# Sixteen experts: loads issued in rotation of twelve places, the tensor engine's groups in a fixed order, the branch behind them marked

## The chip, the cores and the metric

One core of one Trainium2 chip. The metric is the device time of one execution in microseconds (us); the kernel before took 1063.79 us, the median of three runs.

## The reference, cut to what matters

A first block (retention, a recurrent unit, a feed-forward part) and a second block (three attentions, a hierarchical mixture of experts) over 256 tokens of width 1024. The change lies in the last part of the second block, the experts. Each of 256 tokens goes to 2 of 16 experts; an expert has three weights, 1024x256 (gate), 1024x256 (up) and 256x1024 (down), all in float32:

```python
hid = silu(einsum('nd,edf->nef', hf, w_gate)) * einsum('nd,edf->nef', hf, w_up)
hid = hid * combine[..., None]
out = einsum('nef,efd->nd', hid, w_down)
```

`combine` holds the weights of the two chosen experts and zero elsewhere.

## The kernel before, in words

Everything up to the router is one long run of matmuls on TensorE; it ends at about 912 us. What follows is `experts`. Tokens are gathered into 64 places per expert (`SLOTS`), and experts are worked in eight pairs p = 0 to 7 (one expert on the left 64 columns of the array, the other on the right).

The work of TensorE falls into groups, each a small function: `gather(h)` (L1449; 32 matmuls that gather the tokens of eight experts, h = 0 or 1), `up(p)` (L1491; gate and up of a pair), `places` (L1472; once), `turn(p)` (L1505 and L1507; transposes), `down(p)` (L1520), `back(p)` (L1534 and L1535; eight matmuls that spread a pair's result over the tokens, each pair of them followed by an addition on VectorE into `y`, L1537). Between `up` and `turn` stands `act_up` (L1498 on ScalarE, L1499 on VectorE); behind `turn` a copy on ScalarE (L1509) that `down` reads; behind `down` the split of its result into two parts, a copy on ScalarE (L298) and a subtraction on VectorE (L299), which `back` reads. The tiles of that split have four buffers, as many as one pair needs. After the last `back` the four quarters of `y` are stored (L1539).

The program is written with a scheduler that lists each engine's instructions anew: what is traced first has priority, but an instruction that the scheduler believes ready earlier is put ahead. Nothing else orders the groups in the kernel before. Once listed, each engine runs its instructions strictly in that order, and so does the queue of SyncE (SP), which issues all loads: a load that waits for its place holds up all loads behind it.

The weights come in 48 loads of 1 MB, numbered here 0 to 47 in the order of use (the code's index less `FIRST`), each as two transfers of 512 KB into the two halves of a place. `up(0)` takes loads 0 to 3; from p = 1 on `up(p)` takes four and `down(p-1)` two: 4 to 7, 8 and 9, 10 to 13, 14 and 15, and so on; `down(7)` takes 46 and 47. Loads 0 to 4 are fetched long ahead into tiles of the pool `big`. The others take places in a rotation of thirteen written in `load` (L244): three in the pool `raw`, three in `hi`, three in `lo`, four in `big`. So loads 5 to 13 are fetched before the experts begin, 14 to 17 want a `big` tile, 18 to 20 `raw`, 21 to 23 `hi`. `get_raw` (L281) traces a load right where its matmuls are traced. The pool `big` has eleven tiles; when the experts begin, six others hold `pl`, `xt`, `xth`, `xtl` and the two halves of `xg[0]`; later `xg[1]` wants two and `y` one.

Ahead of the experts the router's arithmetic runs on VectorE. Meanwhile `busy` (L1330) lets TensorE repeat a matmul whose result nobody uses, `WAIT[0]` = 36 times and then `WAIT[1]` = 5 times. Behind the experts a count is read (L1412) and a branch (`tc.If`, L1413) steps over a fallback for experts with more than 64 tokens; the inputs here don't enter it.

Of the kernel before, what the change touches and what calls it, by code (L numbers as in the profile page):

```python
# [6 lines left out]
F32 = mybir.dt.float32  # L7
# [6 lines left out]
P = 128  # L14
D = 1024
KT = 8
SEQ = 256
# [9 lines left out]
HALF = 1024  # L27
RAW, SPL, BIG, AHEAD, RAWLI, WARM = 6, 6, 11, 2, 1, 10
PRE = (1, 1, 1, 1, 1, 0, 0, 0)
WAIT = (36, 5)  # L30
SLOTS = 64

OFF1 = dict(q=0, k=1024, v=2048, g=3072, li=4096, lg=5120, ga=6144, gb=7168)
# [91 lines left out]
PLAN = _plan()  # L125
FIRST = next(i for i, (key, _) in enumerate(PLAN) if key[0] == "eu")
# [71 lines left out]
class _Build:  # L198
    def __init__(self, nc, tc, ctx, a):
        self.nc, self.tc, self.a = nc, tc, a  # L200
        pool = lambda name, bufs, **kw: ctx.enter_context(tc.tile_pool(name=name, bufs=bufs, **kw))
        self.rawp, self.lop, self.hip = pool("raw", RAW), pool("wlo", SPL), pool("whi", SPL)
        self.cp, self.big, self.tmp = pool("cst", 1), pool("big", BIG), pool("tmp", 2)
        self.sml = pool("sml", 2)
        self.psum = pool("psum", 4, space=bass.MemoryType.PSUM)
        self.cur, self.emitted, self.split, self.raw, self.turn = 0, 0, {}, {}, 0
        self.ahead = AHEAD
        self.running = []
        self.n = 0
# [28 lines left out]
    def load(self, i, big=False):  # L238
        if i in self.raw:
            return  # L240
        pool = None
        if i >= FIRST and not big:

            pool = ("raw", "raw", "raw", "hi", "hi", "hi", "lo", "lo", "lo", "big", "big", "big", "big")[self.turn % 13]  # L244
            self.turn += 1
            big = pool == "big"
        both = self.bigt(shape=(P, 2, HALF)) if big else None
        self.raw[i] = []
        for h, (off, n) in enumerate(PARTS[i]):
            raw = both[:, h, :] if big else None  # L250
            if pool in ("hi", "lo"):
                raw = (self.hip if pool == "hi" else self.lop).tile([P, HALF], F32, name=self.name("exp"), tag=pool)
            self.raw[i].append(self.load_part(off, n, raw))
# [27 lines left out]
    def get_raw(self, *key):  # L281

        i = self.cur
        assert PLAN[i][0] == key and self.emitted == i
        self.cur = self.emitted = i + 1
        self.load(i)
        return self.raw.pop(i)

    def run_ahead(self, n):
# [1030 lines left out]
    def moe(self, xt, xs, logits, squares, keep):  # L1320
# [55 lines left out]
        def table():  # L1376
# [31 lines left out]
            v.tensor_copy(tab[:, :, 16:18], r3.unsqueeze(2).to_broadcast([P, 2, 2]))  # L1408
            self.split_act(tabs[:, :, 0, :], tabs[:, :, 1, :], tab)

        y = self.experts(xt, None, xs, tabs, place, table)
        n = nc.values_load(count[0:1, 0:1], min_val=0, max_val=SEQ)  # L1412
        with ExitStack() as deeper:  # L1413
            for i in range(1, SEQ // SLOTS):
                deeper.enter_context(self.tc.If(n > SLOTS * i))
                self.cur = self.emitted = FIRST
                xth, xtl = self.bigt(F32R, (P, 2, D)), self.bigt(F32R, (P, 2, D))
                for t in range(2):
                    self.split_act(xth[:, t, :], xtl[:, t, :], xt[:, t, :])
                rest = self.s(32, tag="rest")  # L1420
                v.tensor_scalar(rest, place, -float(SLOTS * i), None, op0=ALU.add)
                self.experts(y, y, (xth, xtl), tabs, rest)

    def experts(self, base, y, xs, tab, place, table=None):
# [2 lines left out]
        ident = self.c("ident")  # L1427
        NP, W = NEXP // 2, 8 * SLOTS
        pl = self.bigt(F32R, (P, 2, NEXP * SLOTS))

        def slots(h):
            for t in range(2):
# [7 lines left out]
        xg = {}  # L1440

        def gather(h):
            xg[h] = [self.bigt(shape=(P, 4, W)) for _ in range(2)]
            for k in range(KT):
                ps = self.mm()
                n = 0
                for t in range(2):
                    for x in xs:
                        te.matmul(ps, x[:, t, k * P:k * P + P], pl[:, t, h * W:h * W + W], start=n == 0, stop=n == 3)  # L1449
                        n += 1  # L1450
                dst = xg[h][k // 4][:, k % 4, :]
                if k % 2:
                    v.tensor_scalar(dst, ps, self.p("gffn", k), None, op0=ALU.mult)
                else:
                    act.mul(dst, ps, self.p("gffn", k))

        last = slots(0)
        gather(0)
        if table:
            with self.tc.issue_after(last.ins):  # L1460
                slots(1)
# [5 lines left out]
        def places():  # L1467

            pw = self.sp()
            for p in range(NP):  # L1470
                for t in range(2):
                    te.matmul(pw[:, 36 * p:36 * p + 36], pl[:, t, p * P:p * P + P], tab[:, t, :, :], start=t == 0, stop=t == 1)  # L1472
            pw4 = pw[:, 0:288].rearrange("p (a i e) -> p a i e", a=8, i=2)
            act.copy(cc[:, 0:144].rearrange("p (a e) -> p a e", a=8), pw4[:, :, 1, :])
            for j, half in enumerate((slice(0, SLOTS), slice(SLOTS, P))):
                v.tensor_tensor(cw[half, :], pw[half, 0:304].rearrange("p (a e) -> p a e", a=8)[:, :, j],
                                cc[half, :].rearrange("p (a e) -> p a e", a=8)[:, :, j], op=ALU.add)
            v.tensor_tensor(cr, pw4[:, :, 0, 16], cc[:, 0:144].rearrange("p (a e) -> p a e", a=8)[:, :, 16], op=ALU.add)
# [3 lines left out]
        def up(p):  # L1482

            ps = self.mm()
            h, o = p // 4, (p % 4) * P
            for i in range(4):
                ws = self.get_raw("eu", p, i)
                for kc in range(2):
                    k = 2 * i + kc
                    for j, w in enumerate(ws):  # L1490
                        te.matmul(ps[j * SLOTS:j * SLOTS + SLOTS, :],  # L1491
                                  xg[h][k // 4][:, k % 4, o + j * SLOTS:o + j * SLOTS + SLOTS],
                                  w[:, kc * 512:kc * 512 + 512], start=k == 0, stop=k == KT - 1)
            return ps

        def act_up(p, ps):
# [5 lines left out]
        def turn(p):  # L1502
            th, pt = hid.pop(p), self.sp()
            for b in range(2):
                te.transpose(pt[:, b * P:b * P + P], th[:, b * P:b * P + P], ident)  # L1505
            for t in range(2):
                te.transpose(pt[:, SEQ + t * P:SEQ + t * P + P], pl[:, t, p * P:p * P + P].bitcast(F32), ident)  # L1507
            hf, pb = self.t(SEQ), self.t(SEQ, F32R)
            act.copy(hf, pt[:, 0:SEQ])  # L1509
            v.tensor_copy(pb, pt[:, SEQ:512])  # L1510
            hid[p], back_[p] = hf, pb

        def down(p):
            hf = hid.pop(p)
            pd = [self.mm() for _ in range(2)]
            for k in range(2):
                ws = self.get_raw("ed", p, k)
                for b in range(2):
                    for j, w in enumerate(ws):
                        te.matmul(pd[b][j * SLOTS:j * SLOTS + SLOTS, :], hf[:, k * P + j * SLOTS:k * P + j * SLOTS + SLOTS],  # L1520
                                  w[:, b * 512:b * 512 + 512], start=k == 0, stop=k == 1)
            outs[p] = []
            for b in range(2):
                oh, ol = self.t(512, F32R), self.t(512, F32R)
                self.split_act(oh, ol, pd[b])
                outs[p].append((oh, ol))

        def back(p, y):

            pb = back_.pop(p)  # L1530
            for b, (oh, ol) in enumerate(outs.pop(p)):
                for t in range(2):
                    ps = self.sp()
                    te.matmul(ps, pb[:, t * P:t * P + P], oh, start=True, stop=False)  # L1534
                    te.matmul(ps, pb[:, t * P:t * P + P], ol, start=False, stop=True)  # L1535
                    c = slice(b * 512, b * 512 + 512)
                    v.tensor_tensor(y[:, t, c], ps, (base if p == 0 else y)[:, t, c], op=ALU.add)  # L1537
                    if p == NP - 1:
                        nc.sync.dma_start(self.a["out"][t * P:t * P + P, c], y[:, t, c])  # L1539

        for p in range(NP + 1):
            if p < NP:
                ps = up(p)
                if p == 0:
                    places()
                act_up(p, ps)
            if p == 1:
                gather(1)
            if p == 2 and y is None:
                y = self.bigt(shape=(P, 2, D))  # L1550
            if p:
                turn(p - 1)
            if 2 <= p < NP:
                back(p - 2, y)
            if p:
                down(p - 1)
        back(NP - 2, y)
        back(NP - 1, y)
        return y


# [76 lines left out]
```

## Time and profile before

| what | us |
|---|---|
| median of three runs (1061.39 to 1063.85) | 1063.79 |
| the profiled execution | 1061.6 |
| its span, first to last instruction | 1059.8 |
| TensorE busy | 1041.5 (98%) |
| experts, from the first matmul of `gather(0)` to the span's end | 913.4 to 1059.8 |

How to read it: instructions of one engine run one after another; an entry of the chain of waits is work or a wait that the end of the program hangs on. A matmul's end is modelled, so the start of the next is what tells, and TensorE's busy share is an upper bound. `L1491` is line 1491. PEld is the loading of a matmul's stationary operand, SPq, PEldq and so on are the sequencers of the engines.

### The profile page before, as it was taken

What the parts mean: (1) busy time and instruction counts of PE and PEld (TensorE: products, weight loads), DVE (VectorE), ACT (ScalarE), POOL (GpSimd) and SP (SyncE); (2) the same over time, 40 slices, a digit from 0 to 9 for tenths busy, and PEclk for the clock granted to TensorE, in tenths of its full rate; (3) what the DMA queues carried; (4) which work ended last, traced back from release to release, by engine and by line L of the source; (5) the groups of instructions that cost most, each with busy time, mean ns of one, the idle gap of its engine ahead of it and who ended that gap; (6) DMA issues with size and microseconds to landing.
All of it is one profiled execution on the core that took longest, in us unless ns stands there. A gap on an engine that the chain in (4) does not pass through costs nothing.

```text
span 1059.8 us, 19451 instructions
## 1 busy us (share of the span) xinstructions
PE 1041.5 (98%) x7806; PEld 938.2 (89%) x7806; DVE 688.8 (65%) x1271; ACT 521.9 (49%) x928; POOL 36.9 (3%) x58
## 2 busy tenths in 40 slices
PE   9999999999999999999999999999999999999995
PEld 8999998899999999999999899999989999753332
DVE  7798977576776666576697466787567675423333
ACT  6578454464455444455575556565456553221101
POOL 3200000000000000000101000000000000000000
PEclk9999999999999999999999999999999999999998
DMA  8644563356555555566427643545555476359981
GB/s 326 231 155 164 181 210 111 119 159 200 179 181 183 190 183 171 183 186 198 139 81 218 191 148 121 198 141 181 182 174 180 130 289 252 146 181 416 412 340 43
DMA packets 57474, 203.32 MB, mean 192 GB/s; under 512 B 6416, under 2 KB 7824, under 8 KB 57248
## 3 DMA queue, kind: packets, MB, share of 16 engines
q1 hardware_dynamic: 57232, 201.91, 55.8%
q8 instruction: 63, 1.03, 0.4%
q14 instruction: 35, 0.29, 0.1%
q10 hardware_dynamic: 144, 0.09, 0.0%
HBM read 200.92 MB, written 1.05 MB: 191 GB/s over the span
## 4 chain that ended last, share of the span: by engine, by line
PE 96%; DMA 1%; DVE 1%; ACT 1%; issue 0%; SPq 0%; POOL 0%; DVEq 0%; ACTq 0%; POOLq 0%
PE mm L342 23%; PE mm L341 23%; PE mm L343 23%; PE mm L1491 5%; PE mm L1520 3%; PE mm L380 2%; PE mm L382 2%; PE mm L381 2%; PE mm L1449 1%; PE sp L402 1%; DMA big<-w 1%; PE sp L1534 1%; PE sp L639 1%; PE sp L640 1%; PE sp L1535 1%; PE mm L523 1%
## 5 line engine op out<-in xcount | busy, mean ns | idle before, releaser
L341 PE MATMUL mm<-big,hi 128*128 128x256 f32 (+1 forms) x2024 | 576.0, 285 | 0.0
L342 PE MATMUL mm<-big,hi 128*128 128x256 f32 (+1 forms) x2024 | 571.9, 283 | 0.0
L343 PE MATMUL mm<-big,lo 128*128 128x256 f32 (+1 forms) x2024 | 570.4, 282 | 0.0
L268 ACT ACTIVATE hi<-raw 128x1024 fp32r<-128x1024 f32 (+1 forms) x279 | 292.6, 1052 | 293.3 <-PE mm L342 163.7
L269 DVE TENSOR_TENSOR lo<-raw,hi 128x1024 fp32r<-128x1024 f32 (+1 forms) x279 | 338.6, 1215 | 119.1 <-ACT hi L268 115.8
L341 PEld LDWEIGHTS mm<-big,hi 128*128 128x128 f32 x2024 | 381.8, 189 | 1.7 <-issue 1.0
L342 PEld LDWEIGHTS mm<-big,hi 128*128 128x128 f32 x2024 | 381.8, 189 | 0.7 <-DVE big L302 0.2
L343 PEld LDWEIGHTS mm<-big,lo 128*128 128x128 f32 x2024 | 382.2, 189 | 0.0
L396 POOL TENSOR_TENSOR sml<-sml,keep 128x2 f32<-128x2 f32 (+4 forms) x17 | 19.4, 1142 | 675.6 <-DVE sml L841 189.9
L1537 DVE TENSOR_TENSOR big<-sp,big 128x512 f32<-128x512 f32 x32 | 20.3, 684 | 19.9 <-PE sp L1535 19.9
L1498 ACT ACTIVATE tmp<-mm,sml 128x256 f32<-128x256 f32 x8 | 3.8, 473 | 56.1 <-PE mm L1491 56.1
L380 PE MATMUL mm<-hi,big 128*128 128x512 f32 (+1 forms) x80 | 29.9, 374 | 0.0
L382 PE MATMUL mm<-lo,big 128*128 128x512 f32 (+1 forms) x80 | 29.7, 372 | 0.0
L381 PE MATMUL mm<-hi,big 128*128 128x512 f32 (+1 forms) x80 | 29.6, 370 | 0.0
L1491 PE MATMUL mm<-big,big 128*64 128x512 f32 x112 | 27.7, 598 | 0.0
L298 ACT ACTIVATE tmp<-mm 128x512 fp32r<-128x512 f32 x16 | 9.2, 596 | 35.1 <-PE mm L1520 35.1
L299 DVE TENSOR_TENSOR tmp<-mm,tmp 128x512 fp32r<-128x512 f32 x16 | 10.8, 690 | 23.4 <-ACT tmp L298 23.2
L1491 PE MATMUL mm<-exp,big 128*64 128x512 f32 x96 | 23.7, 596 | 0.0
L1499 DVE SCALAR_TENSOR_TENSOR tmp<-mm,sml,tmp 128x256 f32<-128x256 f32 x8 | 3.9, 483 | 30.4 <-ACT tmp L1498 30.4
L298 ACT ACTIVATE big<-tmp 128x256 fp32r<-128x256 f32 x46 | 18.2, 407 | 5.8 <-DVE tmp L689 3.2
L1491 PEld LDWEIGHTS mm<-big,big 128*64 128x64 f32 x112 | 7.9, 136 | 14.9 <-issue 14.2
L1491 PEld LDWEIGHTS mm<-exp,big 128*64 128x64 f32 x96 | 7.1, 137 | 13.8 <-issue 13.2
(391 smaller groups left out, 1139.4 us busy)
## 6 DMA issues: line engine op xcount, KB each, us to landing
raw<-w SPq DMA_DIRECT2D x289, 512.0 KB, 3.6
exp<-w SPq DMA_DIRECT2D x38, 512.0 KB, 10.1
big<-w SPq DMA_DIRECT2D x34, 512.0 KB, 10.0
raw<-w SPq DMA_DIRECT2D x16, 448.0 KB, 3.2
big<-xT SPq DMA_DIRECT2D x4, 272.0 KB, 4.5
big<-xT SPq DMA_DIRECT2D x1, 1024.0 KB, 5.8
big<-memT SPq DMA_DIRECT2D x1, 1024.0 KB, 5.7
out<-big SPq DMA_DIRECT2D x4, 256.0 KB, 4.1
```

Source lines behind the costliest of these rows:

```text
L268: nc.scalar.activation(hi[:, :n], raw[:, :n], AF.Copy)
L269: nc.vector.tensor_tensor(lo[:, :n], raw[:, :n], hi[:, :n].bitcast(F32), op=ALU.subtract)
L298: nc.scalar.activation(hi, src, AF.Copy)
L341: nc.tensor.matmul(ps[:m, :n], wh, rh, start=k == 0, stop=False)
L342: nc.tensor.matmul(ps[:m, :n], wh, rl, start=False, stop=False)
L343: last = nc.tensor.matmul(ps[:m, :n], wl, rh, start=False, stop=k == nt - 1)
L380: nc.tensor.matmul(ps[:, :w], xh[:, k, c], wh, start=k == 0, stop=False)
L381: nc.tensor.matmul(ps[:, :w], xl[:, k, c], wh, start=False, stop=False)
L382: nc.tensor.matmul(ps[:, :w], xh[:, k, c], wl, start=False, stop=k == last)
L1491: te.matmul(ps[j * SLOTS:j * SLOTS + SLOTS, :], xg[h][k // 4][:, k % 4, o + j * SLOTS:o + j * SLOTS + SLOTS], w[:, kc * 512:kc * 512 + 512 ...
L1520: te.matmul(pd[b][j * SLOTS:j * SLOTS + SLOTS, :], hf[:, k * P + j * SLOTS:k * P + j * SLOTS + SLOTS], w[:, b * 512:b * 512 + 512], start= ...
L1537: v.tensor_tensor(y[:, t, c], ps, (base if p == 0 else y)[:, t, c], op=ALU.add)
```

## The change

Five things. Rotation: `load` uses twelve places in place of thirteen (three `big` in place of four), and `get_raw` traces not only its own load but all up to eleven ahead. Order: every group of TensorE's is traced inside `issue_after` of the group before it, which lets the scheduler put its matmuls nowhere but behind the last one of that group; it is an order of issue and adds no wait. The sequence itself is that of the loop before but for the end: `turn(7)` comes ahead of `down(6)`, and `down(7)` ahead of `back(6)`. `gather(0)` is traced after the table of weights in place of before it. Marking: `mark_branch_hint_location("done")` ahead of the experts and a label on the branch. Filling: `WAIT[0]` is 31 in place of 36. The line that sets `turn` and `ring` inside the branch belongs to the fallback and is not run.

```diff
-WAIT = (36, 5)
+WAIT = (31, 5)
...
-            pool = ("raw", "raw", "raw", "hi", "hi", "hi", "lo", "lo", "lo", "big", "big", "big", "big")[self.turn % 13]
+            pool = ("raw", "raw", "raw", "hi", "hi", "hi", "lo", "lo", "lo", "big", "big", "big")[self.turn % self.ring]
...
-        self.load(i)
+        for j in range(i, min(len(PLAN), i + self.ring) if i >= FIRST else i + 1):
+            self.load(j)
...
+        self.tc.mark_branch_hint_location("done")
         y = self.experts(xt, None, xs, tabs, place, table)
...
-                deeper.enter_context(self.tc.If(n > SLOTS * i))
+                deeper.enter_context(self.tc.If(n > SLOTS * i, label="done" if i == 1 else None))
                 self.cur = self.emitted = FIRST
+                self.turn, self.ring = 0, 9
...
         last = slots(0)
-        gather(0)
         if table:
...
-        for p in range(NP + 1):
-            if p < NP:
-                ps = up(p)
-                if p == 0:
-                    places()
-                act_up(p, ps)
+        def then(f, *args):
+            if not chain:
+                return f(*args)
+            with self.tc.issue_after(chain[-1].ins):
+                return f(*args)
+
+        then(gather, 0)
+        for p in range(NP):
+            ps = then(up, p)
+            if p == 0:
+                then(places)
+            act_up(p, ps)
             if p == 1:
-                gather(1)
+                then(gather, 1)
             if p == 2 and y is None:
                 y = self.bigt(shape=(P, 2, D))
             if p:
-                turn(p - 1)
-            if 2 <= p < NP:
-                back(p - 2, y)
+                then(turn, p - 1)
+            if p > 1:
+                then(back, p - 2, y)
+            if p == NP - 1:
+                then(turn, p)
             if p:
-                down(p - 1)
-        back(NP - 2, y)
-        back(NP - 1, y)
+                then(down, p - 1)
+        then(down, NP - 1)
+        then(back, NP - 2, y)
+        then(back, NP - 1, y)
```

Each group function now ends with `chain.append(mm)`, mm being its last matmul.

## Rows read from the trace of the kernel before

**Rows 1.** Busy time by stretch: start:end, length, engines, then clock, DMA share, GB/s.
```profile
921.00:928.00 7.00, 7.00 (x33) 2.21 (x32) 0.75 (x1) 0.00 (x0) 0.00 (x0) 1.00 0.00 0
...
980.80:993.70 12.90, 12.90 (x64) 5.17 (x60) 4.63 (x9) 2.04 (x4) 0.00 (x0) 1.00 1.03 413
```

**Rows 2.** Chain of waits, first groups: start us, us, engine and line.
```profile
913.38 7.70 PE mm L1449 x32
921.08 7.02 PE mm L1491 x32
928.10 1.89 PE sp L1472 x16
929.99 7.02 PE mm L1491 x32
937.00 7.65 PE mm L1449 x32
```

**Rows 3.** The same chain, a pair whose groups stand unbroken.
```profile
980.82 6.87 PE mm L1491 x32
987.69 0.37 PE sp L1505 x2
988.06 0.22 PE sp L1507 x2
988.28 0.23 PE sp L1534
...
990.13 3.58 PE mm L1520 x16
```

**Rows 4.** The same chain, where groups are broken up, and its last down.
```profile
1006.61 2.57 PE mm L1491 x10
...
1016.94 1.92 PE mm L1491 x8
...
1019.25 0.37 ACT tmp L1509
...
1045.67 1.96 PE mm L1520 x8
```

**Rows 5.** Waits of the load queue, 880 to 1062: total us, times, longest.
```profile
SPq L258 <- PE mm L1491: 20.3, 8, 16.4
```

**Rows 6.** Timeline of loads and of the matmuls that waited: start, us, engine.
```profile
933.60 4.24 SPq L258 DMA_DIRECT2D raw<-w  x6
...
951.91 6.88 SPq L258 DMA_DIRECT2D big<-w  x8
...
959.70 5.70 PE L1520 MATMUL mm<-big,tmp 128*64 128x512 f32 x16 [0.74 <-DMA big<-w]
```

**Rows 7.** The page: an issue's KB and its median us to landing.
```profile
raw<-w SPq DMA_DIRECT2D x289, 512.0 KB, 3.6
```

**Rows 8.** Timeline of the filling and of the selection that ends it.
```profile
909.02 3.12 PE L1330 MATMUL mm<-big 128*128 128x256 f32 x24
...
911.13 0.19 DVE L1361 TENSOR_TENSOR keep<-tmp 128x32 fp32r<-128x32 f32 x1
...
911.98 0.17 PE L1366 MATMUL sp<-keep,keep 128*128 128x16 f32 x1
```

**Rows 9.** Timeline of the end.
```profile
1048.24 1.29 DVE L299 TENSOR_TENSOR tmp<-mm,tmp 128x512 fp32r<-128x512 f32 x2 [0.96 <-ACT tmp L298]
...
1049.52 2.48 DVE L1537 TENSOR_TENSOR big<-sp,big 128x512 f32<-128x512 f32 x4
```

**Rows 10.** Lines 1539 and 1413: ns min/median/max, first and last start us.
```profile
L1539 SPq DMA_DIRECT2D out<-big x4: 338/868/1602, 1050.2 to 1052.9; - x4
...
L1413 SPq EVENT_SEMAPHORE  x8: 17/17/17, 1057.8 to 1058.4; - x8
...
L1413 PEldq COMPARE_BRANCH  x1: 3858/3858/3858, 1050.2 to 1050.2; - x1
...
L1413 DVEq EVENT_SEMAPHORE  x1: 21/21/21, 1055.8 to 1055.8; - x1
```

More of the change, by code (lines that the diff above doesn't have):

```diff
@@ L205, in __init__ @@
         self.psum = pool("psum", 4, space=bass.MemoryType.PSUM)
-        self.cur, self.emitted, self.split, self.raw, self.turn = 0, 0, {}, {}, 0
+        self.cur, self.emitted, self.split, self.raw, self.turn, self.ring = 0, 0, {}, {}, 0, 12
         self.ahead = AHEAD
@@ L1429, in experts @@
         pl = self.bigt(F32R, (P, 2, NEXP * SLOTS))
+        chain = []
         def slots(h):
@@ L1448, in gather @@
                     for x in xs:
-                        te.matmul(ps, x[:, t, k * P:k * P + P], pl[:, t, h * W:h * W + W], start=n == 0, stop=n == 3)
+                        mm = te.matmul(ps, x[:, t, k * P:k * P + P], pl[:, t, h * W:h * W + W], start=n == 0, stop=n == 3)
                         n += 1
@@ L1455, in gather @@
                     act.mul(dst, ps, self.p("gffn", k))
+            chain.append(mm)
         last = slots(0)
-        gather(0)
         if table:
@@ L1471, in places @@
                 for t in range(2):
-                    te.matmul(pw[:, 36 * p:36 * p + 36], pl[:, t, p * P:p * P + P], tab[:, t, :, :], start=t == 0, stop=t == 1)
+                    mm = te.matmul(pw[:, 36 * p:36 * p + 36], pl[:, t, p * P:p * P + P], tab[:, t, :, :], start=t == 0,
+                                   stop=t == 1)
+            chain.append(mm)
             pw4 = pw[:, 0:288].rearrange("p (a i e) -> p a i e", a=8, i=2)
@@ L1490, in up @@
                     for j, w in enumerate(ws):
-                        te.matmul(ps[j * SLOTS:j * SLOTS + SLOTS, :],
-                                  xg[h][k // 4][:, k % 4, o + j * SLOTS:o + j * SLOTS + SLOTS],
-                                  w[:, kc * 512:kc * 512 + 512], start=k == 0, stop=k == KT - 1)
+                        mm = te.matmul(ps[j * SLOTS:j * SLOTS + SLOTS, :],
+                                       xg[h][k // 4][:, k % 4, o + j * SLOTS:o + j * SLOTS + SLOTS],
+                                       w[:, kc * 512:kc * 512 + 512], start=k == 0, stop=k == KT - 1)
+            chain.append(mm)
             return ps
@@ L1506, in turn @@
             for t in range(2):
-                te.transpose(pt[:, SEQ + t * P:SEQ + t * P + P], pl[:, t, p * P:p * P + P].bitcast(F32), ident)
+                mm = te.transpose(pt[:, SEQ + t * P:SEQ + t * P + P], pl[:, t, p * P:p * P + P].bitcast(F32), ident)
+            chain.append(mm)
             hf, pb = self.t(SEQ), self.t(SEQ, F32R)
@@ L1519, in down @@
                     for j, w in enumerate(ws):
-                        te.matmul(pd[b][j * SLOTS:j * SLOTS + SLOTS, :], hf[:, k * P + j * SLOTS:k * P + j * SLOTS + SLOTS],
-                                  w[:, b * 512:b * 512 + 512], start=k == 0, stop=k == 1)
+                        mm = te.matmul(pd[b][j * SLOTS:j * SLOTS + SLOTS, :],
+                                       hf[:, k * P + j * SLOTS:k * P + j * SLOTS + SLOTS],
+                                       w[:, b * 512:b * 512 + 512], start=k == 0, stop=k == 1)
+            chain.append(mm)
             outs[p] = []
@@ L1534, in back @@
                     te.matmul(ps, pb[:, t * P:t * P + P], oh, start=True, stop=False)
-                    te.matmul(ps, pb[:, t * P:t * P + P], ol, start=False, stop=True)
+                    mm = te.matmul(ps, pb[:, t * P:t * P + P], ol, start=False, stop=True)
                     c = slice(b * 512, b * 512 + 512)
@@ L1539, in back @@
                         nc.sync.dma_start(self.a["out"][t * P:t * P + P, c], y[:, t, c])
-        for p in range(NP + 1):
-            if p < NP:
-                ps = up(p)
-                if p == 0:
-                    places()
-                act_up(p, ps)
+            chain.append(mm)
+        def then(f, *args):
[9 more added lines that the diff above has]
+            act_up(p, ps)
             if p == 1:
-                gather(1)
+                then(gather, 1)
             if p == 2 and y is None:
```

## The prediction

> **What bounds the kernel now.** I read the busy time by stretch first, from 905 us on, because the change touches nothing earlier. [...] The load queue is not steady: while `up(0)` runs it moves 0 GB/s, and from some 951 us on it is full at about 413 GB/s [rows 1]. So two things could set the end: TensorE's own list, or the loads. The chain of waits says which. Its first groups are plain matmul work: `gather(0)` 7.70, `up(0)` 7.02, `places` 1.89, `up(1)` 7.02, `gather(1)` 7.65 us, together 31.27 us from 913.38 to 944.65 [rows 2]. Later a pair whose groups stand in one piece takes 6.87 for `up`, 0.37 + 0.22 for `turn`, eight times 0.23 = 1.85 for `back` (988.28 to 990.13) and 3.58 for `down`: 12.89 us, and the stretch 980.8 to 993.7 shows TensorE without a pause and the load queue full beside it [rows 1, 3]. That is what a pair must cost.
>
> Most pairs cost more, since the scheduler has cut their groups to fit others between. In p = 6 `up`, `turn` and `back` run from 1006.61 to 1016.94 + 1.92 = 1018.86, 12.25 us for 9.31 us of work: 2.9 lost to changes between kinds of matmuls. Then the copy on ScalarE that `down` reads runs until 1019.62, because `turn` was put so early that its copy came to stand behind `act_up`, which waits for all of `up`: 0.8 us lost [rows 4]. Pairs 3 and 7 are cut in the same way.
>
> The loads add to it. One wait of the load queue for `up` lasted 16.4 us [rows 5]. Behind it went loads 18 to 20 at 933.60, and loads 14 to 17, which are needed first, only at 951.91; `down(1)` started at 959.70, 0.74 us late, and took 5.70 us for 3.58 of work [rows 3, 6]. That costs 0.74 + 2.1 = 2.8 us. So TensorE's list bounds this stage, the loads only once.
>
> **The change part by part.**
>
> Filling, 36 to 31. The last 24 repeats ran to 909.02 + 3.12 = 912.14, while the selection that the next real matmul reads was done at 911.13 + 0.19 = 911.32 and that matmul started at 911.98 [rows 8]. One repeat is 2.88 / 24 = 0.12 us by their starts in the chain; five are 0.6 us. The slack is 911.98 - 911.32 = 0.66. Gain 0.6 us, all of it on the path; `gather(0)` starts at 912.78.
>
> Order. With every group whole, I add the rows up. 912.78 + 31.27 = 944.05 at the end of `gather(1)`. `turn(0)` 0.59, then `down(0)` must wait for the copy of 0.37 and its signals: 0.45; here alone no `back` stands between [rows 3, 4]. `down(0)` 3.6: 948.7. Six pairs (p = 2 to 7) at 12.9: 1026.1. `turn(7)`, moved up into p = 7, 0.55: 1026.7; its `act_up` has the 2.4 us of `turn(6)` and `back(5)` as cover (without them a wait like the 0.8 us of p = 6). `down(7)` 3.6: 1030.3. Before, `down(7)` ended at 1045.67 + 1.96 = 1047.63 [rows 4], so TensorE gains 17.3 us there, but it still owes `back(6)`, which the kernel before had done by then.
>
> The new end is therefore VectorE's. Behind `down(7)` it has four additions for `back(6)`, 2.48, two subtractions of the split, 1.29, and four additions for `back(7)`, 2.48: 6.25 us, from about 0.75 us after `down(7)`, when the first pair of `back(6)` is through: 7.0 us. Before it was 1049.52 + 2.48 - 1047.63 = 4.4 us [rows 9]. Bounds: 5.0, if `back(6)` is worked off while TensorE still ends `down(7)`, and 7.8, if the split waits once more for one of its four buffers (0.8 like the copy of [rows 4]). I take 7.0, since every piece of it has its row. Last addition at 1037.3 instead of 1052.0: 14.7 us, the filling included. The copy that `down` needs costs nothing in pairs 2 to 7, since `back` covers it, as in the unbroken pair, where `down` follows `back` at once (988.28 + 1.85 = 990.13) [rows 3]; without that cover it costs the 0.8 us of p = 6 each time.
>
> Rotation. Load j may now start when load j - 12 is used up, in the order of use. Load 14 goes when the first quarter of `up(0)` is through, 920.5 + 1.75 = 922.2, instead of 951.91. It and the two behind it ask for `big` tiles before `xg[1]` and `y` do, because they are traced earlier; `xg[1]` then takes the places of loads 3 and 4, free at about 931, before `gather(1)` writes at 936.5. Load 17 waits for load 5 (933), load 20 for load 8, the first half of `down(0)`: 944.05 + 1.04 + 1.8 = 946.9. From there on a load takes 1.0486 MB / 413 GB/s = 2.54 us and lands some 4.9 us after it starts (3.6 to the landing of a transfer [rows 7], 1.27 for the second half). Load 14 lands at 927 and is needed at 958; load 22 at 957, needed at 974.5; load 47 starts at 946.9 + 27 x 2.54 = 1015.5, lands at 1020.4 and is needed at 1028.5. Places come free in time as well (load 32 would start at 977.4, load 20 is used by 972.5). So the loads cost nothing, with 8 us to spare at the tightest point. One place fewer in the rotation takes 2.5 us of that lead. What is queued behind a waiting load are later loads alone; the four stores come after them all.
>
> The table ahead of `gather(0)`: its small operations come before some evacuations on VectorE. Four banks of PSUM cover nearly 4 us of that, so I put it at 0, bounds 0 to 0.5.
>
> Marking. Its own instruction is not in the trace: by the nearest rows between 0.02 us (a semaphore instruction) and 3.9 us (a branch that stalls) [rows 10]; I take 0, for it doesn't jump. What it can give back: TensorE's branch took 3.86 us and VectorE's next instruction came at 1055.8, though its last work ended at 1052.0. Neither is on the path: SP's last wait ends at 1057.8, with the last store's landing [rows 10]. But two of the four stores took up to 1.6 us to issue where the shortest took 0.34, in the same 3 us; if the branches' fetching slowed them, up to 2.0 us return. The rows cannot say: I take 1.0, halfway, and keep 0 and 2.0. [...]
>
> Sum: 14.7 + 1.0 = 15.7 us. The profiled execution had a span of 1059.8, 7.8 of it behind the last addition, and took 1061.6; the new span is 1037.3 + 7.8 - 1.0 = 1044.1, the time 1045.9. The median shown is 2.2 us above the profiled execution, so I predict 1063.8 - 15.7 = 1048.1 us.
>
> **The rivals.**
>
> Waits come to light (1053.7). A fixed order lets nothing fill a pause. If in each of seven pairs `down` waits 0.8 us for its copy as in [rows 4], 5.6 us are lost. For it: that is what p = 6 did. Against it: in the unbroken pair of [rows 3] the same sequence ran without a pause.
>
> The first `big` load stands until `gather(1)` ends (1052.4). If `xg[1]` and `y` still get the first free tiles, load 14 must have that of `xth` or `xtl`, free at 944.05, and everything waits behind it. Then 34 loads at 2.54 follow: the last one starts at 944.05 + 83.8, lands at 1032.8, `down(7)` ends at 1034.6 and not 1030.3. For it: loads 14 to 17 did come last before [rows 6]. Against it: the new order of tracing.
>
> Slower: the load queue stands until `xt` is read (1067.7). `xt` is the operand of the additions of `back(0)`; were load 14 given its tile, it would start at about 959.4, the last load would land at 959.4 + 83.8 + 4.9 = 1048.1, `down(7)` end at 1049.9, 19.6 us later than forecast. It decides from a first load at about 959 on; at 955 the kernel is no slower. Against it: other tiles come free 14 us sooner.
>
> The order has no effect (1063.2). If the scheduler lists the groups as before, the filling's 0.6 us is left. Against it: each group's matmuls hang on the last one of the group before.
>
> **How the numbers follow.** Forecast 0.72, its own range 1045.5 to 1051 (tail 5.0 to 7.8, marking 0 to 2.0, and the spread of the runs shown, some 2 us). Waits 0.12, first `big` load 0.08, no effect 0.04, slower 0.04. Faster by over 0.3% (3.2 us, about what can be told from no change): 0.72 + 0.12 + 0.08 = 0.92; within: 0.04; slower: 0.04. The range 1044 to 1054 takes in the forecast with its bounds and the first two rivals.
>
> **What would show it.** In the chain of waits: `up` in one piece of 32 and eight `back` matmuls in a row for every pair, 12.9 us each; `down(7)` ending near 1030. In the loads: the first `big` load at about 922, the last one issued by 1016, none of TensorE's waits ended by a load. At the end: additions and the split on VectorE for some 6 us after `down(7)`; TensorE's branch short and all four stores issued in 0.3 us if the marking works. It would be wrong if `down` waits for ScalarE in every pair, if the first load comes after 944, or if TensorE's list before 905 us is no longer the same.

## The result and the profile after

The changed kernel took 1044.82 us (median; 1044.04 to 1045.75), the kernel before, run beside it, 1062.59 us (1060.61 to 1063.85): a ratio of 0.9835, 95% interval 0.9814 to 0.9855. The gain of 17.8 us lies a little above the 15.7 forecast. The time is inside the range of 1044 to 1054; it is 0.7 us under the forecast's own 1045.5 to 1051, which was counted from a before of 1063.79.

The profiled execution of after took 1044.04 us with a span of 1042.3, that of before 1061.6 with 1059.8. The 17.5 us between the spans, cut at the same four points of both traces (us from the span's start):

| | before | after | difference | forecast |
|---|---|---|---|---|
| start of the filling | 907.4 | 904.8 | -2.6 | 0 |
| filling, to the start of `gather(0)` | 6.0 | 5.5 | -0.5 | -0.6 |
| `gather(0)` to the end of the last addition | 138.6 | 123.8 | -14.8 | -14.1 |
| from there to the end | 7.8 | 8.2 | +0.4 | -1.0 |

The chain of waits of after, start us, us, engine and line:

```profile
910.27 7.64 PE mm L1453 x32
917.91 7.02 PE mm L1497 x32
924.93 1.89 PE sp L1476 x16
926.82 7.02 PE mm L1497 x32
933.84 7.65 PE mm L1453 x32
...
942.38 3.65 PE mm L1528 x16
946.04 6.87 PE mm L1497 x32
...
955.34 3.58 PE mm L1528 x16
958.92 6.87 PE mm L1497 x32
...
1020.26 7.07 PE mm L1528 x32
1027.33 0.42 PE sp L1544
```

The first five groups are those of [rows 2], of equal length to 0.1 us. Then comes what [rows 4] did not have: `up` is one piece of 32 in every pair, and a `down` begins each 12.9 us (955.34, 968.24, 981.14, 994.03, 1006.92), the pace of the unbroken pair of [rows 3]. `down(6)` and `down(7)` stand together as one piece of 32 that ends at 1027.33. From 0.7 us later on VectorE works without a pause to the last addition; its timeline (in brackets: how long the engine had waited, and for what):

```profile
1028.02 1.29 DVE L1547 TENSOR_TENSOR big<-sp,big 128x512 f32<-128x512 f32 x2 [2.19 <-PE sp L1545]
1029.23 1.28 DVE L300 TENSOR_TENSOR tmp<-mm,tmp 128x512 fp32r<-128x512 f32 x2
1030.42 3.67 DVE L1547 TENSOR_TENSOR big<-sp,big 128x512 f32<-128x512 f32 x6
```

These are eight additions and the two subtractions of the split, so the end is VectorE's.

Busy time by stretch in after; the columns are those of [rows 1]. `up(0)`, and a later pair:

```profile
918.00:925.00 7.00, 7.00 (x34) 2.19 (x32) 0.70 (x1) 0.00 (x0) 0.00 (x0) 1.00 0.57 189
978.00:991.00 13.00, 13.00 (x64) 5.18 (x60) 4.65 (x8) 2.04 (x4) 0.00 (x0) 1.00 1.03 409
```

While `up(0)` runs, the load queue now moves 189 GB/s, where it stood at 0. The timeline of the load queue shows the loads in the order of use, in runs of six or twelve transfers of 512 KB:

```profile
919.82 4.32 SPq L258 DMA_DIRECT2D big<-w  x6
930.43 4.25 SPq L258 DMA_DIRECT2D raw<-w  x6
944.34 9.39 SPq L258 DMA_DIRECT2D exp<-w  x12
954.30 7.75 SPq L258 DMA_DIRECT2D big<-w  x6
```

The `big` loads that went last at 951.91 [rows 6] go first at 919.82. The queue's waits from 877 us on (total, times, longest) have lost the one of 16.4 us [rows 5]; 6.5 is the longest left on that line:

```profile
SPq L258 <- PE mm L1497: 20.5, 13, 6.5
```

And the end: the stores, and what the engines do at the branch, in the columns of [rows 10].

```profile
L1549 SPq DMA_DIRECT2D out<-big x4: 338/368/1857, 1032.3 to 1035.5; - x4
...
L1415 SPq EVENT_SEMAPHORE  x8: 17/17/17, 1039.0 to 1039.6; - x8
...
L1415 PEldq COMPARE_BRANCH  x1: 4238/4238/4238, 1032.3 to 1032.3; - x1
```

TensorE's branch takes 4.24 us, 3.86 before [rows 10], and one store still takes 1.86 us to issue. Of the marking nothing is to be seen here; a run below says why.

### The profile page after: what moved, and what is told of

Same layout as the page of the kernel before. It is cut to its first block, busy times and chain, and to the rows that moved or that the text cites. A ratio compares the mean times of both kernels' runs of the same rounds, so it can differ in the third digit from the quotient of the medians.

```text
span 1042.3 us, 19441 instructions
## 1 busy us (share of the span) xinstructions
PE 1027.4 (99%) x7801; PEld 934.2 (90%) x7801; DVE 687.5 (66%) x1271; ACT 522.6 (50%) x928; POOL 36.9 (4%) x58
## 4 chain that ended last, share of the span: by engine, by line
PE 97%; DVE 1%; ACT 0%; DMA 0%; issue 0%; POOL 0%; DVEq 0%; ACTq 0%; POOLq 0%
PE mm L342 23%; PE mm L343 23%; PE mm L344 23%; PE mm L1497 5%; PE mm L1528 3%; PE mm L381 2%; PE mm L383 2%; PE mm L382 2%; PE mm L1453 1%; PE sp L403 1%; PE sp L640 1%; PE sp L1544 1%; PE sp L641 1%; PE sp L1545 1%; PE mm L524 1%; PE sp L410 0%
## 5 line engine op out<-in xcount | busy, mean ns | idle before, releaser
L1497 PE MATMUL mm<-raw,big 128*64 128x512 f32 x96 | 21.3, 592 | 0.0
L1497 PE MATMUL mm<-exp,big 128*64 128x512 f32 x96 | 21.1, 592 | 0.0
L1497 PEld LDWEIGHTS mm<-raw,big 128*64 128x64 f32 x96 | 6.9, 137 | 13.7 <-issue 13.4
```

Source lines behind the costliest of these rows:

```text
L1497: mm = te.matmul(ps[j * SLOTS:j * SLOTS + SLOTS, :], xg[h][k // 4][:, k % 4, o + j * SLOTS:o + j * SLOTS + SLOTS], w[:, kc * 512:kc * 512 ...
```

## The experiments

Each edit is shown against the changed kernel unless it says otherwise. "Stage" is the time from the start of `gather(0)` to the end of the last addition in the run's trace: 138.6 us before, 123.8 after. It leaves out what varies ahead of the stage, by which single times here differ up to 3.4 us; the last run of this section comes back to that. A time given without a range is that of one execution.

**The order alone.**

```diff
-WAIT = (31, 5)
+WAIT = (36, 5)
...
-            pool = ("raw", "raw", "raw", "hi", "hi", "hi", "lo", "lo", "lo", "big", "big", "big")[self.turn % self.ring]
+            pool = ("raw", "raw", "raw", "hi", "hi", "hi", "lo", "lo", "lo", "big", "big", "big", "big")[self.turn % 13]
...
-        for j in range(i, min(len(PLAN), i + self.ring) if i >= FIRST else i + 1):
-            self.load(j)
+        self.load(i)
...
-        self.tc.mark_branch_hint_location("done")
...
```

> The change's fixed order of groups alone; loads in the rotation of thirteen, traced where they are used, filling of 36, no marking. Theory (the order is most of the gain): pairs of 12.9 us as in the changed kernel, loads 14 to 17 again only near 945 to 950, so that down(1) waits 1 to 4 us for them and the last down about 3 us for its load: about 1048 to 1050. Rival (the loads are most of the gain): 1057 or more.

1053.4 us (1051.81 to 1055.06), ratio 0.9916 [0.9897, 0.9935]; stage 131.6. So the order without the loads gives 9 us, not 12 to 15, and not the 5.5 or less of the rival. The timeline of this run says where the rest stays:

```profile
953.31 7.48 SPq L258 DMA_DIRECT2D big<-w  x8
...
961.72 5.36 PE L1525 MATMUL mm<-big,tmp 128*64 128x512 f32 x14 [2.94 <-DMA big<-w]
...
968.98 2.35 PE L1494 MATMUL mm<-big,big 128*64 128x512 f32 x8 [1.03 <-DMA big<-w]
```

The `big` loads go at 953.31 as they did before at 951.91. `down(1)` waits 2.94 us for them and takes 5.2 us in place of 3.6; `up(3)` waits too. TensorE's granted clock in this stretch was 0.85; in after it was 1.00 over the same 963 to 972 us:

```profile
963.00:972.00 9.00, 7.76 (x27) 2.61 (x27) 1.38 (x2) 1.19 (x2) 0.00 (x0) 0.85 1.03 417
```

What `up(3)` waits for in the end are the loads, though, as the chain of this run shows:

```profile
960.46 11.03 DMA big<-w
...
971.53 5.36 PE mm L1494 x22
```

`turn(2)` starts 63.2 us after `gather(0)` (976.83) where in after it is 55.5 (965.79): 7.7 us, which is the whole difference between the two stages (131.6 - 123.8 = 7.8). I had put the loads' price at 2.8 us for the old order and at 1 to 4 for this one; a fixed order has nothing to put into the pause, so it pays the wait in full. The 3 us expected at the last `down` did not come: behind `turn(2)` this run is as fast as after.

**The loads alone**, the edit against the kernel before:

```diff
-            pool = ("raw", "raw", "raw", "hi", "hi", "hi", "lo", "lo", "lo", "big", "big", "big", "big")[self.turn % 13]
+            pool = ("raw", "raw", "raw", "hi", "hi", "hi", "lo", "lo", "lo", "big", "big", "big")[self.turn % self.ring]
...
-        self.load(i)
+        for j in range(i, min(len(PLAN), i + self.ring) if i >= FIRST else i + 1):
+            self.load(j)
```

> The rotation of twelve with loads traced up to eleven ahead, alone; groups of TensorE free for the scheduler as before, filling of 36, no marking. Theory (order is most): the first big load at about 923, down(1) no longer waits (2.8 us less), the groups are still cut: 1058 to 1061. Rival (loads are most): 1050 or less.

1052.04 us (1051.60 to 1052.88), ratio 0.9904 [0.9889, 0.9919]; stage 128.8. By my theory the scheduler would go on cutting groups and the loads would give back little more than the one stall. That fell (1058 to 1061 expected); the 1050 or less of the rival was not reached either. The chain of waits of this run:

```profile
975.17 6.87 PE mm L1493 x32
...
984.48 3.58 PE mm L1522 x16
...
997.37 3.58 PE mm L1522 x16
...
1014.49 1.00 PE mm L1493 x2
...
1019.14 1.00 PE mm L1493 x2
...
1020.81 5.31 PE mm L1493 x22
```

With no order written out, every `up` and `down` stands whole until 1013.90, the later ones at 12.9 us a pair. Only `up(7)`, `down(6)` and `down(7)` are cut, in the way that [rows 4] showed for p = 6. So most of the cutting before went away with the earlier tracing of the loads; since the scheduler lists what it believes ready, I take it that it had believed the loads late and filled the gap with other groups. That belief itself is not in a trace. The run changes two things at once, twelve places for thirteen and loads traced ahead; no run parts them. Alone, the parts give 9.1 us (order) and 10.4 (loads) against the before beside them (1062.46), 19.5 in sum where the whole change gives 17.8. On top of the loads the rest of the change brings 1052.0 - 1044.8 = 7.2 us, 5.0 of them in the stage (128.8 - 123.8), where the order keeps the last groups whole.

**Three and six places fewer in the rotation.**

```diff
-        self.cur, self.emitted, self.split, self.raw, self.turn, self.ring = 0, 0, {}, {}, 0, 12
+        self.cur, self.emitted, self.split, self.raw, self.turn, self.ring = 0, 0, {}, {}, 0, 9
```

(and 6 for the second run)

> The changed kernel with a rotation of nine places (no big ones). By the changed kernel's trace the last load lands at 1020.9 and its second half is needed at 1025.5; three places fewer let three loads more wait for down(0), 7.7 us later: 3 us lost, from the first matmul of gather(0) to the last addition 126.8 us in place of 123.8. By the prediction's arithmetic (8 us to spare) nothing is lost.

> The changed kernel with a rotation of six places. Theory (the loads run at their full rate from down(0) on, and each place is worth 2.56 us of lead): 7.7 us more than with nine, about 134.5 us from gather(0) to the last addition. Rival (six places hold the loads up in lockstep with TensorE): over 140 us.

With nine places 1047.85 us, stage 126.7; with six 1057.42, stage 134.4. TensorE's waits for loads, with nine and then with six places (total us, times, longest):

```profile
PEld mm L1497 <- DMA raw<-w: 3.7, 7, 1.1
```

```profile
PEld mm L1497 <- DMA raw<-w: 14.6, 25, 1.5
```

In after's trace load 47 landed at 1020.85 and was needed at 1025.5: 4.7 us of lead. Three places at 2.54 us (the prediction's time of one load at the full queue) take 7.6 of it, so 2.9 late; measured 126.7 - 123.8 = 2.8. Six take 15.2, so 10.5 late; measured 10.6. From nine to six a place cost 2.6 us. Once the lead is gone the stage is as long as the loads make it, and with six places 10.6 of the 14.8 us that the stage had gained are lost again.

**The filling at 36.**

```diff
-WAIT = (31, 5)
+WAIT = (36, 5)
```

> The changed kernel with 36 repeats in the filling. From the first repeat to the first matmul of gather(0) 6.01 us as in the kernel before, in place of 5.51; all later stretches as in the changed kernel.

1047.52 us. The filling lasted 6.01 us as in before, against 5.51 in after, and the stage stayed at 123.9. The term is 0.5 us. This run took 3.5 us more than the profiled execution of after, and the other 3.0 do not lie here: its filling began 3.2 us later, its end was 0.2 shorter.

**The marking left out.**

```diff
-        self.tc.mark_branch_hint_location("done")
...
-                deeper.enter_context(self.tc.If(n > SLOTS * i, label="done" if i == 1 else None))
+                deeper.enter_context(self.tc.If(n > SLOTS * i))
```

> The changed kernel without the marking and without the label. The built program has the same instructions, so all stretches behind the filling must come out as in the changed kernel: 123.8 us from gather(0) to the last addition, TensorE's branch 4 us.

1046.34 us, stage 123.9. The two built programs hold the same instructions, one by one: written with a name alone, the marking put nothing into the program here, and after's trace has no such instruction among its 19441. TensorE's branch took 4.48 us here and 4.24 in after. That two executions of one program differ by 2.3 us gives a measure of what varies between them.

**The marking with engines named.**

```diff
-        self.tc.mark_branch_hint_location("done")
+        self.tc.mark_branch_hint_location("done", hint="LikelyTaken", engines=list(mybir.ALL_ENGINES))
```

> The changed kernel, but the marking names the engines, so that the built program holds five hint instructions (the changed kernel's holds none). Theory A (fetching at the branch slows the stores): TensorE's branch falls from 4.2 us to under 0.3, all stores issue in about 0.35 us, 1042.5 to 1043.8. Theory B (fetching is hidden): the branch is short or not, the time stays within 0.5 us of 1044.8.

1043.98 us (1043.79 to 1046.67), ratio 0.9835 [0.9819, 0.9851]; stage 123.9. Now there is an instruction on each engine, at the program's start, and the branch is short. One of the five, and the branch:

```profile
L1655 PEldq BRANCH_PREFETCH_HINT  x1: 50/50/50, 0.8 to 0.8; - x1
```

```profile
L1549 SPq DMA_DIRECT2D out<-big x4: 338/368/2152, 1034.0 to 1037.5; - x4
...
L1415 PEldq COMPARE_BRANCH  x1: 398/398/398, 1034.0 to 1034.0; - x1
```

TensorE's branch fell from 4.24 to 0.40 us. What it had spent that time on is not shown: three packets of the DMA queues of kind `instruction` start while it lasts in after (1032.3 to 1036.5), three in before (1050.2 to 1054.1), but nothing ties the branch to them. What reaches the end is less, because SP waits for the last store's landing meanwhile: its next semaphore instruction comes at 1040.4 us here, 1039.0 in after, where the branch was over by 1036.6. From the last addition to the end it is 6.6 us here. In the eight traces of this study with the fixed order and no such instruction it is 6.9 to 8.3, mean 7.7. So by the traces the marking, where it is emitted, is worth about 1.1 us, with 0.3 and 1.7 as the ends; the medians with and without it (1043.98, 1044.82) don't tell them apart. And the slow store is there as before, 2.15 us, beside a branch of 0.40, while in the run without the marking no store took over 0.39 us beside a branch of 4.48: in these runs a long branch on TensorE is not what makes it slow.

**The last two spreads summed in PSUM**, aimed at the new end: `back(6)` and `back(7)` are accumulated in the same four banks, so VectorE has four additions instead of eight.

```diff
+        def last_two(y):
...
+                        te.matmul(ps, pb[:, t * P:t * P + P], oh, start=p == NP - 2, stop=False)
+                        mm = te.matmul(ps, pb[:, t * P:t * P + P], ol, start=False, stop=p == NP - 1)
...
+                        if p == NP - 1:
+                            v.tensor_tensor(y[:, t, c], ps, y[:, t, c], op=ALU.add)
...
-        then(back, NP - 2, y)
-        then(back, NP - 1, y)
+        then(last_two, y)
```

> The changed kernel, but back(6) and back(7) add up in the same four banks of PSUM, so that VectorE has four additions behind down(7) and not eight. Theory (the end is VectorE's list): from the end of down(7) to the last addition 5.4 us in place of 6.8, so about 1043.4. Rival (the end hangs on TensorE or on the split's buffers): 6.8 us as before, 1044.8.

1044.58 us (1043.27 to 1045.38), ratio 0.9831 [0.9817, 0.9845]; stage 122.6, 1.2 us shorter. Four additions are 2.48 us [rows 9]; the chain says why half of it stays:

```profile
1021.78 7.07 PE mm L1528 x32
1028.85 0.43 PE sp L1586
...
1031.34 0.69 DVE tmp L300
1032.03 1.20 DVE big L1590 x2
...
1033.74 0.68 DVE big L1590
```

From `down(7)`'s end at 1028.85 to the split's second subtraction at 1031.34 the path now goes through `back(6)` on TensorE and a copy on ScalarE, 2.5 us; the last addition ends 5.6 us after `down(7)` in place of 6.8. The bound has moved from VectorE to the handover between three engines.

**`turn(7)` put behind `down(6)`**, which takes the cover away that the change gives it.

```diff
-            if p == NP - 1:
-                then(turn, p)
             if p:
                 then(down, p - 1)
+        then(turn, NP - 1)
         then(down, NP - 1)
```

> The changed kernel with turn(7) behind down(6), as in the kernel before. down(7) then stands right behind the copy that it reads and waits 0.45 us as down(0) does: 124.3 us from gather(0) to the last addition in place of 123.8.

1047.82 us; stage 124.8, 1.0 longer. In the chain `down(7)` waits for the copy on ScalarE, which stands behind the split's first copy:

```profile
1023.16 3.67 PE mm L1528 x16
1026.83 0.58 ACT tmp L299
1027.41 0.00 issue
1027.41 0.38 ACT tmp L1517
1027.80 0.04 issue
1027.84 3.71 PE mm L1528 x16
```

A pause of 1027.84 - 1026.83 = 1.0 us, twice the 0.45 expected. It is `down`'s wait for its copy, as in [rows 4], where it cost 0.8 us; there the copy stood behind `act_up`, here behind the split. It shows what the wait costs where no `back` covers it, and bears out why pairs 2 to 7 run without it in after.

**Both additions of the end together**, the sum in PSUM and the marking with engines.

```diff
-        self.tc.mark_branch_hint_location("done")
+        self.tc.mark_branch_hint_location("done", hint="LikelyTaken", engines=list(mybir.ALL_ENGINES))
...
-        then(back, NP - 2, y)
-        then(back, NP - 1, y)
+        then(last_two, y)
```

> The changed kernel with both additions: back(6) and back(7) summed in PSUM, and the marking with engines named. If both effects of the traces hold (1.2 us from gather(0) to the last addition, 1.9 us from the last landing to the end), 1041.5 to 1043; if they don't add up to the end of the program, 1044 or more.

1042.24 us (1040.83 to 1046.24), the lowest median of all. Its ratio to the before beside it, 0.9831 [0.9810, 0.9852], is no different from after's, so the total doesn't prove it better; the trace shows where it is shorter: stage 122.7 (-1.1) and 6.6 us from the last addition to the end in place of 8.2 (-1.5). Here no store was slow to issue:

```profile
L1591 SPq DMA_DIRECT2D out<-big x4: 332/335/352, 1032.0 to 1033.8; - x4
```

**The kernel before once more.**

> The kernel before once more, for a second trace. If the 2.6 us by which the changed kernel reaches the filling earlier are the execution's and not the change's, this trace reaches it anywhere between 904.7 and 908; from gather(0) to the last addition 138.6 us again.

1062.12 us, the filling from 907.5 on, stage 139.0, and two slow stores of 1.39 and 1.60 us as in [rows 10]. The times up to the filling differ between the executions of this study, from 904.8 us (after) to 908.2 (the run without the marking), though TensorE's list up to there is the same. Half of it or more can be one short stretch. Busy time by stretch in before, in after, and in the run without the marking, which is after's own program:

```profile
525.00:542.00 17.00, 16.68 (x125) 14.85 (x124) 15.80 (x43) 11.66 (x24) 0.00 (x0) 1.00 0.29 100
542.20:545.60 3.40, 3.40 (x20) 3.40 (x18) 3.33 (x18) 1.65 (x6) 0.00 (x0) 0.51 0.51 154
```

```profile
542.20:545.60 3.40, 3.40 (x31) 3.40 (x31) 3.30 (x16) 2.98 (x7) 0.00 (x0) 1.00 0.27 111
```

```profile
542.20:545.60 3.40, 3.40 (x16) 3.09 (x15) 3.37 (x17) 2.37 (x8) 0.00 (x0) 0.55 0.48 154
```

At 542 us the granted clock over 3.4 us is 0.51 in before, 0.55 in the same program as after, and 1.00 in after. Set side by side matmul by matmul, before falls 1.5 us behind after here, and 1.2 us between 315 and 438 us, at a granted clock of 1.00, and hardly anywhere else:

```profile
340.00:443.00 103.00, 103.00 (x869) 103.00 (x868) 64.43 (x90) 48.88 (x71) 0.00 (x0) 1.00 0.56 179
```

```profile
340.00:443.00 103.00, 103.00 (x876) 103.00 (x875) 65.45 (x90) 49.98 (x74) 0.00 (x0) 1.00 0.57 182
```

869 matmuls in before against 876 in after in the same 103 us. The 1.2 us (1.1 to 1.2) came in all of the thirteen traces but after's and that of both additions, the 1.5 us in six (before twice, the order alone, the loads alone, the marking left out, `turn(7)` behind `down(6)`). A third part, 0 to 2.0 us, came ahead of 100 us. What sets them was not shown. The run without the marking, after's own program, has all three, so the 2.6 us need not belong to the change: its gain without them, between the two traces, is 14.9 us, a little under the 15.4 at which the interval of the ratio begins. How much of the 17.8 of the medians is such variation can't be settled with these runs.

## Why the prediction was right, point by point

**What bounds the stage: the sum was right, its cause was not.** "So TensorE's list bounds this stage, the loads only once" is the step that failed. It read the cuts of [rows 4] as the scheduler's own habit and gave the loads 2.8 us. The loads alone gave 10.4 us, most of it by pairs that became whole; the order alone left over 7 us of stalls on loads. The loads alone are enough for 12.9 us a pair up to p = 6, and the order keeps the last pairs whole. My total came out because after has both, which as far as this step goes is luck: the expectations drawn from it for one part alone were wrong (loads 1058 to 1061, measured 1052.0; order 1048 to 1050, measured 1053.4).

**Order.** Every term of the new list held. `gather(0)` to the end of `gather(1)` took 31.2 us (31.27 forecast), `turn(0)` with the wait of `down(0)` 0.9 (1.04), from `down(0)`'s end at 946.04 to `down(7)`'s at 1027.33 81.3 us (six times 12.9, and 0.55 and 3.6: 81.5). The pause of 0.8 us for ScalarE's copy didn't come in pairs 2 to 7, and came with 1.0 us where the cover was taken away; the rival of 1053.7 falls with that.

**The tail on VectorE.** 7.0 us was forecast from `down(7)`'s end to the last addition's, 6.8 measured: right in kind too, as VectorE's timeline shows and the sum in PSUM, which took four additions out and shortened it to 5.6. The split did wait for its buffers, the wait of the bound of 7.8 (ScalarE's copies in after start at 1028.26 and 1029.18, both released by `back(6)`), but VectorE had additions to do meanwhile.

**Rotation.** No wait of TensorE on a load in after is over 0.4 us, and the first `big` load went at 919.82, where the prediction's 922.2 less the 2.6 us of the earlier start is 919.6; so the two rivals that let it stand, at 1052.4 and at 1067.7, fall. The lead was mis-sized: 4.7 us, not 8. Load 20 came as forecast, but the 27 loads behind it took 71.5 us to land (949.36 to 1020.85), 2.65 each and not 2.54, since a few came 0.4 to 1.1 us later than the even pace; that is 2.9 of the missing 3.4. "One place fewer takes 2.5 us of that lead" was right (2.6), but two places, not three, are enough to use it up.

**Filling.** 0.5 us, for 0.6 forecast, on the path as said.

**Table ahead of `gather(0)`.** 0, as forecast: the first five groups kept their lengths.

**Marking.** 1.0 us was forecast, halfway between 0 and 2.0, on the supposition that the branches' fetching slows the stores. No run shows that term, nor that a branch waits for a fetch; what the runs showed is a branch of 0.40 us in place of 4.24 where the marking names the engines, and by the traces some 1.1 us at the end. Two things failed. The marking as written emitted no instruction. And the slow store, 2.15 us, stood beside that short branch. The end section came out 0.4 us longer, not 1.0 shorter: from the last addition to the last store's landing 1.5 us less (one slow store, not two), from there to the end 1.9 more. The prediction took SP's wait for the landing as cover for every branch. For TensorE's 4.24 us that holds: it was over by 1036.6 us, and the last store landed at 1038.5. But in after SP goes on only 0.6 us after the landing and then stands 1.3 us among its last semaphore instructions; with the engines named both pauses are gone (1.9 us from landing to end, against 3.8). What SP waits for there is open. Its own branch stands ahead of the landing (1035.91, 0.05 us), no row names another cause, and in before the same way took 1.9 us without any marking.

**Upstream.** The sum assumed equal times up to 905 us and would have been wrong, by its own words, if TensorE's list had changed there. The list did not change and the time did, by 2.6 us. The forecast also carried over the 2.2 us by which the shown median stood above before's profiled execution; after's median stands 0.8 above its own. Without the upstream part the predicted 15.7 us compare with 14.9.

**No effect (1063.2)** falls with the chain of after: each group is whole and follows the one written before it.

## What to carry to other kernels

Groups cut to pieces on the critical engine can be the mark of a late operand rather than of a bad order: try the earlier issue alone before crediting an order, and issue loads in the order of use so that none that is needed late stands ahead of one that is needed soon. When the order of an engine is fixed, nothing fills its pauses any more, so the loads' lead has to be counted in places and microseconds, and a hand-over without cover costs its full length, 1.0 us at `down(7)` here. A mark in the source is not an instruction in the program: look for it in the trace before giving it a price.

## What the runs showed of the hardware

Over 3.4 us at 542 us the granted clock was 0.51 in before, 0.55 in the run without the marking and 1.00 in after, which has the same program as that run; TensorE was busy for 16.68 of the 17 us ahead of it in all three. Before fell 1.5 us behind after there; no row seen here tells what decides it. One or two of the four stores took 1.4 to 2.2 us to issue in before (1.38 and 1.60), in after (1.86) and with the engines named (2.15, beside a branch of 0.40), where the others took 0.34 to 0.40; the longest took 0.39 in the run without the marking, after's own program, and 0.35 with both additions. The cause is open. And from the last landing to the end it took 3.8 us in after and 2.4 in the run without the marking, 1.9 with the branch announced on all engines, but 1.9 as well in before, without any announcement; what SP waits for in the longer cases is open.
